# Row blocks 2 and 3, right half, by Strassen instead of plainly, in a fused matmul and RMSNorm kernel

## Chip, cores, metric

The kernel runs on one core of a Trainium2 chip (trn2). The metric is the device time in microseconds (us) of one execution. Every time quoted for a kernel is a median of runs.

In this kernel TensorE (PE in the traces) does the matmuls, ScalarE (ACT) and VectorE (DVE) the copies, sums, squares and scalings, GpSimd (POOL) issues nearly all loads, and SyncE (SP) the DMA transposes and nearly all stores. "Granted clock" is the share of its full clock that the trace records for TensorE. A bank is a piece of the memory into which matmuls accumulate.

## The reference

```python
def setup_inputs():
    m, k, n = 2048, 2048, 2048
    return {"a": randn(m, k), "b": randn(k, n), "gamma": randn(n), "eps": 1e-5}   # float32

def reference(a, b, gamma, eps):
    x = np.matmul(a, b)
    rms = np.sqrt(np.mean(x ** 2, axis=-1, keepdims=True) + eps)
    return (gamma * x / rms).astype(np.float32)
```

## The kernel before

The 2048 rows of the output are 16 row blocks of 128 rows. Its 2048 columns are four chunks of 512; chunks 0, 1 are the left half, 2, 3 the right half.

- **Head.** Row blocks 0 to 3 are multiplied plainly in bf16 while B streams in: the left halves in a first pass, the right halves in a second one.
- **Groups.** Row blocks 4 to 15 are six groups `g = 2..7` of two blocks. A group is done in two half-groups (`j = 0`, `j = 1`), left and right. Each is a one-level Strassen: 7 products of 8 matmuls instead of 8 products.
- **Preparation.** While a group is multiplied, the two blocks of the next one are loaded, their row norms taken, scaled to fp16 by ScalarE, and transposed by DMA.

The half-group: `hooks` are pieces of other work put between its steps.

```python
def group_half(g, j, hooks):
    ...                                        # x11, x12, x21, x22: chunks of the x tiles of this half
    t = x22
    at_hook(0)
    p2, p5 = new_bank(), new_bank()
    product(g, j, 2, p2)
    c = spare if (g, j) == (G0, 0) else t      # G0 = 2
    nc.scalar.copy(out=c, in_=p2)              # must be done before product 4 adds into p2
    last_squares()
    at_hook(1)
    product(g, j, 5, p5)
    nc.vector.tensor_tensor(out=t, in0=p5, in1=c, op=ALU.add)   # before product 3 adds into p5
    at_hook(2)
    ...                                        # product 1; t = p1 - t
    at_hook(3)
    product(g, j, 4, p2, start=False)
    nc.scalar.copy(out=x21, in_=p2)
    square(rb, x21)
    ...                                        # x11 = t + x21
    at_hook(4)
    product(g, j, 3, p5, start=False)
    nc.scalar.copy(out=x12, in_=p5)
    ...                                        # squares, sums, then products 7 and 6
```

The eight x tiles of the head are used again for the groups: a tile must first be scaled (`finish`) and stored. The loads of the blocks after next are paced:

```python
def x_tile(mb, h):
    ...
        if n < 8:
            slot = n
        else:
            g = n // 4
            slot = ((0, 4, 1, 5), (0, 1, 4, 5))[g // 2 % 2 == 0][n % 4] + 2 * (g % 2)
    ...

def load_after(g, mb):
    wait_for(x_chunk(2 * g + 1, 1)[:, 0:1])    # GpSimd reads one column: waits for x22 of j = 0
    load_block(mb)

def hooks_of(g, j):
    ...
    def apply(mb):
        row_apply(mb)                          # scale to fp16
        transpose_dma(mb)                      # issued by SyncE
    if j == 0:
        if g == G0:
            ...                                # row_factor of blocks 6 and 7, row_norm of 7, apply of 6
            hook(2, finish, 1)
            ...
            hook(4, apply, nxt + 1)
            hook(4, finish, 2)
        else:
            hook(0, row_factor, nxt)
            hook(1, apply, nxt)
            ...
            hook(1, row_norm, nxt + 1)
            hook(4, apply, nxt + 1)
    else:
        ...
        if g + 2 < NG:
            hook(0, load_after, g, nxt + 2)
            hook(0, load_block, nxt + 3)
            hook(5, row_norm, nxt + 2)
```

Of the kernel before, what the change touches and what calls it, by code (L numbers as in the profile page):

```python
# [17 lines left out]
def kernel(  # L18
# [32 lines left out]
    stat_pool = ctx.enter_context(tc.tile_pool(name="stat_pool", bufs=8))  # L51
# [25 lines left out]
    spare = head_at.rearrange("p t r m -> p (t r m)")[:, K:2 * K].bitcast(FP32)[:, 0:CH]  # L77

    def a16_slot(mb):

        if mb < HB + 2:
            return x_slot[HB + 1 + 2 * (mb % 2)].bitcast(FP16)
        flat = head_at.rearrange("p t r m -> p (t r m)").bitcast(FP16)
        return flat[:, (2 + mb % 2) * K:(3 + mb % 2) * K]
# [27 lines left out]

    def load_block(mb):
        a32[mb] = a_pool.tile([P, K], FP32, name="a32")
        nc.gpsimd.dma_start(out=a32[mb], in_=a[mb * P:(mb + 1) * P, :])
# [8 lines left out]
    identity_f = consts.tile([P, P], FP32, name="identity_f")  # L124
# [4 lines left out]
    nc.vector.memset(warm, 0.0)  # L129
    identity = consts.tile([P, P], BF16, name="identity")  # L130
# [43 lines left out]
    def transpose_half(mb, g):  # L174
        bank = ps_t.tile([P, CH], FP32, name="tbank")
# [7 lines left out]
        nc.vector.tensor_copy(out=at(mb)[:, g * 8:(g + 1) * 8, :], in_=view)  # L183
# [8 lines left out]
    def new_msq(mb):  # L192
        msq[mb] = stat_pool.tile([P, NCH + 1], FP32, name="msq")
        n_sq[mb] = 0

    for mb in range(HB):
        new_msq(mb)
        nc.gpsimd.memset(msq[mb][:, NCH:], float(eps))
# [27 lines left out]
    def row_apply(mb):  # L226
        a16[mb] = a16_slot(mb)
        if mb < HB + 2:
            nc.vector.tensor_scalar_mul(out=a16[mb], in0=a32.pop(mb), scalar1=factor.pop(mb))
# [5 lines left out]
    def quarter(g, r, c):  # L235
        return at(2 * g + r)[:, c::2, :]

    def a_sums(g, which):
# [3 lines left out]
        for s in which:  # L242
            x, y, op = terms[s]
            nc.vector.tensor_tensor(out=s_sum[s], in0=x, in1=y, op=op)  # L244
# [11 lines left out]
    def b_sum_7(j, kp):  # L256

        b21, b22 = (b_quarter(j, kp, 1, c) for c in range(2))
        nc.vector.tensor_tensor(out=b21, in0=b21, in1=b22, op=ALU.add)

    def b_sum_6(j, kp):

        b11, b12 = (b_quarter(j, kp, 0, c) for c in range(2))
        nc.vector.tensor_tensor(out=b12, in0=b12, in1=b11, op=ALU.add)

# [6 lines left out]
    def product(g, j, m, bank, start=True):  # L272
        for kp in range(KP):
            lhsT = {3: quarter(g, 0, 0), 4: quarter(g, 1, 1)}[m] if m in (3, 4) else s_sum[m]
            rhs = {1: lambda: sums[j][:, 0, kp, :], 2: lambda: b_quarter(j, kp, 0, 0),
                   3: lambda: sums[j][:, 1, kp, :], 4: lambda: sums[j][:, 2, kp, :],
                   5: lambda: b_quarter(j, kp, 1, 1), 6: lambda: b_quarter(j, kp, 0, 1),
                   7: lambda: b_quarter(j, kp, 1, 0)}[m]()
            nc.tensor.matmul(bank, lhsT[:, kp, :], rhs,  # L279
                             start=(start and kp == 0), stop=(kp == KP - 1),  # L280
                             skip_group_check=not start)
# [5 lines left out]
    def square(mb, src):  # L287
# [3 lines left out]
        nc.scalar.activation(out=sq[:, 0:CH], in_=src, func=ACTF.Square,  # L291
                             scale=inv_sqrt_n, accum_out=msq[mb][:, c:c + 1])
# [40 lines left out]

    def finish(mb, order=(0, 1)):
        if mb not in rms_of:
            take_rms(mb)
        r = inverse(rms_of.pop(mb))
# [15 lines left out]
    def new_bank():  # L353
        return ps_a.tile([P, CH], FP32, name="acc")

    later = ([("b", kp) for kp in range(5)]
             + [("a", HB), ("b", 5), ("b", 6), ("a", HB + 1), ("b", 7)])

    def load_later(n):
        for _ in range(min(n, len(later))):  # L360
            kind, which = later.pop(0)
            load_b(1, which) if kind == "b" else load_block(which)
# [31 lines left out]

    groups1 = [(r, c) for r in range(HB) for c in range(2)][:-1]
    last1 = (HB - 1, 1)
    banks = {}
    for r in range(HB):
        x_tile(r, 0)
    transpose_first()  # L400
    for kp in range(KP):
# [4 lines left out]
        before = [lambda: transpose_head(kp + 1)] if kp + 1 < KP else []  # L406
        stream(groups1, kp, before, len(groups1) + 5 if kp == 0 else None)
# [3 lines left out]
        if kp > 0:  # L411
            b_sums(0, kp - 1)
    load_later(2)
    b_sums(0, KP - 1)


    def prepare(mb):
        row_norm(mb)
        row_factor(mb)
        row_apply(mb)  # L420

    def b_sums_2(kp):
        b_sums_in_place(0, kp)
        b_sums(1, kp)
        if kp + 1 < KP:
            b_sum_7(1, kp)

    r3 = HB - 1
    squares = groups1 + [last1]
    groups2 = [(r, c) for r in range(HB) for c in (2, 3)][:-1]  # L430
    for kp in range(KP):
        load_later(1)
        before = [lambda: transpose_half(HB, 0)] if kp == 6 else []
        if kp == 7:
            before = [lambda: transpose_half(HB, 1)]
        stream(groups2, kp, before)
        square(squares[kp][0], x_chunk(*squares[kp]))
        if kp == 4:
            prepare(HB)
        if kp == 6:  # L440

            prepare(HB + 1)
        elif kp == KP - 1:
            b_sums_in_place(0, kp - 1)
        else:
            b_sums_2(kp)
# [3 lines left out]


    def squares2(r):
        for c in (2, 3):
            square(r, x_chunk(r, c))

    evict(groups2[0:2], ())
    squares2(0)
# [279 lines left out]
```

## Time and profile before

| | before |
|---|---|
| time | 224.42 us (224.33 to 224.44, 3 runs) |
| span of the profiled run | 222.6 us |
| TensorE (PE) busy | 211.1 us |
| last matmul starts | 214.41 us |

From the page of the kernel before, the share of each engine, and two rows of the 40 equal slices (busy tenths of PE, granted clock in tenths):

```profile
PE 211.1 (95%) x1043; PEld 98.6 (44%) x1043; DVE 161.8 (73%) x324; ACT 129.1 (58%) x272; POOL 24.5 (11%) x49
...
PE   7899999999999999999999999999999999999950
...
PEclk9999999999999999999999999999999999999997
```

PE is full from the third slice to the thirty-eighth. The chain that ended last, in order of time (start, length, what), says the same: from 69.41 us on it is one piece of PE.

```profile
67.26 2.16 PE acc L350 x10
69.41 140.08 PE acc L279 x648
209.50 0.02 issue
```

648 matmuls in 140.08 us are 216 ns each. The waits of PE over the whole run (us in total, times, longest) all lie before 25 us:

```profile
PE acc L138 <- DVE sq L129: 1.5, 1, 1.5
PE tbank L148 <- POOL msq L198: 1.2, 1, 1.2
PE acc L350 <- DMA b<-in_b_dram: 0.4, 1, 0.4
PE tbank L382 <- DVE head_at L170: 0.4, 1, 0.4
```

By stretches of time (length, then busy us and instructions of PE, weight loads, VectorE, ScalarE, GpSimd, then clock, DMA share, GB/s), PE is full while VectorE is almost full as well:

```profile
80.00:90.00 10.00, 10.00 (x48) 4.44 (x46) 9.42 (x18) 7.46 (x17) 1.24 (x3) 1.00 0.97 293
90.00:100.00 10.00, 10.00 (x48) 4.57 (x47) 8.68 (x22) 8.50 (x19) 0.00 (x0) 1.00 0.52 206
100.00:110.00 10.00, 10.00 (x48) 4.49 (x46) 9.22 (x16) 8.69 (x19) 0.11 (x1) 1.00 0.79 248
```

The last lines shown are GpSimd's in group 3: the pacing copy is released by VectorE's write of x22 (L525), and the two loads for group 5 follow.

```profile
109.89 0.18 POOL L121 COPY pace<-x 128x1 f32<-128x1 f32 x1 [20.46 <-DVE x L525]
110.44 1.05 POOL L115 DMA_DIRECT2D a<-in_a_dram  x2 [0.37 <-issue]
```

They do not wait for the second transpose of the group, which lands at 116.38 us, 5.9 us after the loads are issued.

### The profile page before, as it was taken

To read this page: it belongs to the slowest core of one execution; us is meant where nothing else is said; L and a number is where in the kernel's file an instruction comes from. 1 tells how busy PE (TensorE), PEld (TensorE's weight loads), DVE (VectorE), ACT (ScalarE), POOL (GpSimd) and SP (SyncE) were. 2 spreads that over 40 slices of the span, in tenths; PEclk is the share of its full clock that TensorE was granted. 3 is DMA by queue.
4 is the path that set the end of the run, shared out by engine and by line. 5 is a ranking of instruction groups with operands and counts; after the bars stand their busy time and mean duration, and the time that the engine had idled before them with its cause. 6 is when DMAs were issued, how large, how long until landed. Compare 5 with 4: busy or idle time off the path is not lost.

```text
span 222.6 us, 3026 instructions
## 1 busy us (share of the span) xinstructions
PE 211.1 (95%) x1043; PEld 98.6 (44%) x1043; DVE 161.8 (73%) x324; ACT 129.1 (58%) x272; POOL 24.5 (11%) x49
## 2 busy tenths in 40 slices
PE   7899999999999999999999999999999999999950
PEld 2445444444454444444444444444444444444430
DVE  2427557983999989978949298837994589587692
ACT  3110002807698895799646985699478954334570
POOL 7534232300000001000100002000200000000000
PEclk9999999999999999999999999999999999999997
DMA  6999999999973499818889259945994794044045
GB/s 184 223 202 209 203 208 211 212 303 259 327 280 159 188 272 292 310 72 226 276 228 400 58 174 222 366 151 143 246 368 168 97 282 189 0 188 193 0 190 188
DMA packets 36176, 47.13 MB, mean 212 GB/s; under 512 B 21952, under 2 KB 26048, under 8 KB 34496
## 3 DMA queue, kind: packets, MB, share of 16 engines
q0 software_dynamic: 9648, 23.33, 41.6%
q1 hardware_dynamic: 26080, 22.29, 33.0%
q10 hardware_dynamic: 432, 1.31, 2.0%
q8 instruction: 8, 0.13, 0.2%
q14 instruction: 8, 0.07, 0.1%
HBM read 34.60 MB, written 16.78 MB: 231 GB/s over the span
## 4 chain that ended last, share of the span: by engine, by line
PE 83%; DMA 8%; DVE 2%; POOL 2%; issue 1%; ACT 1%; DVEq 0%; ACTq 0%; POOLq 0%
PE acc L279 63%; PE acc L350 18%; DMA b<-in_b_dram 8%; POOL early L106 1%; DVE x L617 1%; POOL b L100 1%; DVE x L620 1%; PE tbank L179 1%; PE tbank L382 1%; PE tbank L165 1%; ACT sq L291 0%; DVEq L732 0%; ACT sq L682 0%; DVE x L690 0%; DVE r L322 0%
## 5 line engine op out<-in xcount | busy, mean ns | idle before, releaser
L279 PE MATMUL acc<-b,s 128*128 128x512 bf16 x376 | 83.3, 379 | 0.0
L279 PEld LDWEIGHTS <-s 128*128 128x128 f16 x472 | 46.2, 98 | 55.7 <-DVE s L244 0.2
L350 PE MATMUL acc<-b,head_at 128*128 128x512 bf16 x240 | 55.1, 379 | 0.6 <-DMA b<-in_b_dram 0.4
L291 ACT ACTIVATE sq<-x 128x512 bf16<-128x512 f32 x62 | 39.1, 631 | 10.9 <-DVE x L520 5.1
L340 DVE SCALAR_TENSOR_TENSOR x<-x,r,gamma_sb 128x1024 f32<-128x1024 f32 x28 | 34.7, 1282 | 0.8
L209 ACT ACTIVATE sq<-a 128x1024 bf16<-128x1024 f32 x24 | 25.4, 1057 | 16.8 <-DMA a<-in_a_dram 16.4
L350 PEld LDWEIGHTS <-head_at 128*128 128x128 bf16 x240 | 22.9, 98 | 26.7 <-issue 1.1
L393 ACT COPY x<-acc 128x512 f32<-128x512 f32 x11 | 5.9, 591 | 25.1 <-PE acc L350 25.1
L231 ACT ACTIVATE head_at<-a,s 128x2048 f16<-128x2048 f32 x10 | 19.9, 1990 | 0.0
L279 PEld LDWEIGHTS <-at_even 128*128 128x128 f16 x96 | 9.4, 98 | 11.5 <-issue 0.4
L279 PEld LDWEIGHTS <-head_at 128*128 128x128 f16 x96 | 9.4, 98 | 11.3
L100 POOL DMA_DIRECT2D b<-in_b_dram x15 | 10.6, 708 | 16.0 <-DMA b<-in_b_dram 13.2
L217 DVE TENSOR_SCALAR s<-norm 128x1 f32<-128x1 f32 x12 | 1.8, 150 | 14.3 <-ACT norm L212 14.2
L244 DVE TENSOR_TENSOR s<-at_even 128x1024 f16<-128x1024 f16 x15 | 9.7, 684 | 2.8 <-DMA at_even<-head_at 2.8
L291 ACT ACTIVATION_READ_ACCUMULATOR sq<-x 128x1 f32 x62 | 11.7, 188 | 0.0
L279 PE MATMUL acc<-t_left,s 128*128 128x512 bf16 x48 | 11.3, 379 | 0.0
L279 PE MATMUL acc<-early,s 128*128 128x512 bf16 x48 | 11.3, 379 | 0.0
L279 PE MATMUL acc<-early,at_even 128*128 128x512 bf16 x48 | 11.0, 379 | 0.0
L279 PE MATMUL acc<-t_left,at_even 128*128 128x512 bf16 x48 | 10.9, 379 | 0.0
L509 ACT COPY x<-acc 128x512 f32<-128x512 f32 x10 | 5.7, 575 | 8.9 <-PE acc L279 8.9
L279 PE MATMUL acc<-t_left,head_at 128*128 128x512 bf16 x48 | 10.8, 379 | 0.0
L279 PE MATMUL acc<-early,head_at 128*128 128x512 bf16 x48 | 10.8, 379 | 0.0
(86 smaller groups left out, 205.8 us busy)
## 6 DMA issues: line engine op xcount, KB each, us to landing
out_dram<-x SPq DMA_DIRECT2D x30, 512.0 KB, 3.1
a<-in_a_dram POOLq DMA_DIRECT2D x12, 1024.0 KB, 8.5
b<-in_b_dram POOLq DMA_DIRECT2D x15, 512.0 KB, 17.1
early<-in_a_dram POOLq DMA_DIRECT2D x7, 256.0 KB, 14.8
early<-in_b_dram ACTq DMA_DIRECT2D x2, 512.0 KB, 5.9
gamma_sb<-in_gamma_dram POOLq DMA_DIRECT2D x1, 1024.0 KB, 19.9
out_dram<-x SPq DMA_DIRECT2D x3, 256.0 KB, 3.5
early<-in_a_dram SPq DMA_DIRECT2D x1, 512.0 KB, 5.7
```

What stands on the lines that cost most here:

```text
L100: nc.gpsimd.dma_start(out=raw[j][kp], in_=b[kp * W2:(kp + 1) * W2, j * HALF:(j + 1) * HALF].rearrange("(t p) n -> p t n", p=P))
L106: nc.gpsimd.dma_start(out=ah(kp), in_=a[0:HB * P, kp * W2:(kp + 1) * W2].rearrange("(r p) k -> p r k", p=P))
L165: nc.tensor.matmul(view[:, t, r, :], ah(kp)[:, r, t * P:(t + 1) * P], identity, is_transpose=True, start=(t == 0 and r == 0), stop=(t == 1 ...
L209: nc.scalar.activation(out=junk, in_=a32[mb][:, h * HALF:(h + 1) * HALF], func=ACTF.Square, scale=2.0 ** -8, accum_out=n2[:, h:h + 1])
L231: nc.scalar.activation(out=a16[mb], in_=a32.pop(mb), func=ACTF.Copy, scale=factor.pop(mb))
L244: nc.vector.tensor_tensor(out=s_sum[s], in0=x, in1=y, op=op)
L279: nc.tensor.matmul(bank, lhsT[:, kp, :], rhs, start=(start and kp == 0), stop=(kp == KP - 1), skip_group_check=not start)
L291: nc.scalar.activation(out=sq[:, 0:CH], in_=src, func=ACTF.Square, scale=inv_sqrt_n, accum_out=msq[mb][:, c:c + 1])
L340: nc.vector.scalar_tensor_tensor(out=x, in0=x, scalar=r, in1=gamma_sb[:, h * HALF:(h + 1) * HALF], op0=ALU.mult, op1=ALU.mult)
L350: nc.tensor.matmul(bank, head_at[:, kt, r, :], head_rhs(c, kt), start=(kt == 0), stop=(kt == KT - 1))
L393: copy(out=x_chunk(*g), in_=banks[g])
L509: nc.scalar.copy(out=x21, in_=p2)
```

## The change

The intent is to save 8 of 928 matmuls of 512 columns (the last eight are run as sixteen of 256): the right half of row blocks 2 and 3, 64 plain matmuls, becomes one more Strassen half of 56. Its products 2, 5 and 1 are streamed with B in the second pass, 4, 3, 7 and 6 follow. To make room in time and memory, more is moved. The core of the diff:

```diff
+def pair_matmul(m, kp): ...            # one matmul of product m of the pair (blocks 2, 3)
 for kp in range(KP):                    # second pass
     load_later(1)
-    stream(groups2, kp, before)         # 7 plain groups a step; the 8th afterwards
+    b_sums(1, kp)
+    stream_right(kp)                    # 4 plain groups, and products 2, 5, 1 of the pair
...                                      # then pair products 4, 3, 7, 6 with the transposes of blocks 4, 5
 def group_half(g, j, hooks):
-    t = x22
+    first = (g, j) == (G0, 0)
+    c, t = (spare if first else (spare[1], spare[1])) if g == G0 else (x22, x22)
     ...                                 # (G0, 0) does product 5 before product 2
 def load_after(g, mb):
-    wait_for(x_chunk(2 * g + 1, 1)[:, 0:1])
+    wait_for(at(2 * g + 3)[:, KT - 1, 0:1])       # the transposed block itself
     load_block(mb)
 ...                                     # g == G0, j == 0 (other hooks left out):
-                hook(2, finish, 1)
-                hook(4, apply, nxt + 1)
-                hook(4, finish, 2)
+                hook(0, finish, 0, (1,))
+                hook(2, apply, nxt)
+                hook(2, finish, 0, (0,))
+                hook(2, apply, nxt + 1)
+                hook(2, pair_sums)
+                hook(2, pair_ends)
+                hook(5, square_half, r2, 1)
+                hook(5, take_rms, r2)
+                hook(5, square_half, r3, 1)
+                hook(7, finish, 1, (1, 0))
```

Cut: five sums of A for the pair, in-place sums of B, the other moved hooks, the square-root table loaded early, A blocks 4 and 5 loaded in halves after all of B, smaller pools. Before, row block 0 was finished ahead of group 2, and blocks 1 and 2 inside its first half-group. After, the finishing of blocks 0 and 1 stands inside that half-group, that of block 2 in the second.

More of the change, by code (lines that the diff above doesn't have):

```diff
@@ L50 @@
     sq_pool = ctx.enter_context(tc.tile_pool(name="sq_pool", bufs=1))
-    stat_pool = ctx.enter_context(tc.tile_pool(name="stat_pool", bufs=8))
+    stat_pool = ctx.enter_context(tc.tile_pool(name="stat_pool", bufs=4))
+    msq_pool = ctx.enter_context(tc.tile_pool(name="msq_pool", bufs=8))
     ps_t = ctx.enter_context(tc.tile_pool(name="ps_t", bufs=1, space=bass.MemoryType.PSUM))
@@ L75 @@
     x_slot = [consts.tile([P, HALF], FP32, name=f"x_{n}") for n in range(8)]
-    spare = head_at.rearrange("p t r m -> p (t r m)")[:, K:2 * K].bitcast(FP32)[:, 0:CH]
+    spare = head_at.rearrange("p t r m -> p (t r m)")[:, K:2 * K].bitcast(FP32)
+    spare = [spare[:, 0:CH], consts.tile([P, CH], FP32, name="t_first")]
     def a16_slot(mb):
-        if mb < HB + 2:
-            return x_slot[HB + 1 + 2 * (mb % 2)].bitcast(FP16)
         flat = head_at.rearrange("p t r m -> p (t r m)").bitcast(FP16)
@@ L111, with load_half @@
     a32 = {}
+    def load_half(mb, h):
+        if h == 0:
+            a32[mb] = a_pool.tile([P, K], FP32, name="a32")
+        nc.gpsimd.dma_start(out=a32[mb][:, h * HALF:(h + 1) * HALF],
+                            in_=a[mb * P:(mb + 1) * P, h * HALF:(h + 1) * HALF])
     def load_block(mb):
@@ L123 @@
     load_head(1)
-    identity_f = consts.tile([P, P], FP32, name="identity_f")
+    identity_f = t_left[:, 2, KP - 1, 0:2 * P].bitcast(FP32)
     make_identity(nc, identity_f)
@@ L129 @@
     nc.vector.memset(warm, 0.0)
+    nc.vector.memset(pace, 1.0)
+    nc.scalar.activation(out=pace, in_=pace, func=ACTF.Sqrt)
     identity = consts.tile([P, P], BF16, name="identity")
@@ L172, with transpose_half @@
     a16 = {}
-    def transpose_half(mb, g):
-        bank = ps_t.tile([P, CH], FP32, name="tbank")
+    def transpose_half(mb, g, own_bank):
+        if own_bank:
+            bank = ps_t.tile([P, CH], FP32, name="tbank")
+        else:
+            bank = ps_a.tile([P, CH], FP32, name="acc")
         view = bank.bitcast(FP16).rearrange("p (g m) -> p g m", m=P)
@@ L182, in transpose_half, with take_transposed @@
             )
-        nc.vector.tensor_copy(out=at(mb)[:, g * 8:(g + 1) * 8, :], in_=view)
+        return view
+    def take_transposed(mb, g, view, copy):
+        copy(out=at(mb)[:, g * 8:(g + 1) * 8, :], in_=view)
     def transpose_dma(mb):
@@ L192, in new_msq @@
     def new_msq(mb):
-        msq[mb] = stat_pool.tile([P, NCH + 1], FP32, name="msq")
+        msq[mb] = msq_pool.tile([P, NCH + 1], FP32, name="msq")
         n_sq[mb] = 0
@@ L197 @@
         new_msq(mb)
+        nc.gpsimd.memset(msq[mb][:, NCH - 1:NCH], 0.0)
         nc.gpsimd.memset(msq[mb][:, NCH:], float(eps))
@@ L235, in quarter, with sum_of, a_sums @@
     def quarter(g, r, c):
+        if g < G0:
+            return head_at[:, c::2, 2 * g + r, :]
         return at(2 * g + r)[:, c::2, :]
-    def a_sums(g, which):
+    def sum_of(g, s):
+        return s_sum[s].bitcast(BF16) if g < G0 else s_sum[s]
+    def a_sums(g, which, lo=0, hi=KP):
         a11, a12, a21, a22 = (quarter(g, r, c) for r in range(2) for c in range(2))
@@ L243, in a_sums @@
             x, y, op = terms[s]
-            nc.vector.tensor_tensor(out=s_sum[s], in0=x, in1=y, op=op)
+            nc.vector.tensor_tensor(out=sum_of(g, s)[:, lo:hi, :], in0=x[:, lo:hi, :],
+                                    in1=y[:, lo:hi, :], op=op)
     def b_quarter(j, kp, r, c):
@@ L254, in b_sums @@
             nc.vector.tensor_tensor(out=sums[j][:, n, kp, :], in0=x, in1=y, op=op)
-    def b_sum_7(j, kp):
-        b21, b22 = (b_quarter(j, kp, 1, c) for c in range(2))
-        nc.vector.tensor_tensor(out=b21, in0=b21, in1=b22, op=ALU.add)
-    def b_sum_6(j, kp):
-        b11, b12 = (b_quarter(j, kp, 0, c) for c in range(2))
-        nc.vector.tensor_tensor(out=b12, in0=b12, in1=b11, op=ALU.add)
     def b_sums_in_place(j, kp):
@@ L270, in b_sums_in_place, with product_matmul, product @@
                                 op=ALU.add)
-    def product(g, j, m, bank, start=True):
-        for kp in range(KP):
-            lhsT = {3: quarter(g, 0, 0), 4: quarter(g, 1, 1)}[m] if m in (3, 4) else s_sum[m]
-            rhs = {1: lambda: sums[j][:, 0, kp, :], 2: lambda: b_quarter(j, kp, 0, 0),
-                   3: lambda: sums[j][:, 1, kp, :], 4: lambda: sums[j][:, 2, kp, :],
-                   5: lambda: b_quarter(j, kp, 1, 1), 6: lambda: b_quarter(j, kp, 0, 1),
-                   7: lambda: b_quarter(j, kp, 1, 0)}[m]()
-            nc.tensor.matmul(bank, lhsT[:, kp, :], rhs,
-                             start=(start and kp == 0), stop=(kp == KP - 1),
-                             skip_group_check=not start)
+    def product_matmul(g, j, m, bank, kp, start=True):
+        lhsT = {3: quarter(g, 0, 0), 4: quarter(g, 1, 1)}[m] if m in (3, 4) else sum_of(g, m)
+        rhs = {1: lambda: sums[j][:, 0, kp, :], 2: lambda: b_quarter(j, kp, 0, 0),
+               3: lambda: sums[j][:, 1, kp, :], 4: lambda: sums[j][:, 2, kp, :],
+               5: lambda: b_quarter(j, kp, 1, 1), 6: lambda: b_quarter(j, kp, 0, 1),
+               7: lambda: b_quarter(j, kp, 1, 0)}[m]()
+        nc.tensor.matmul(bank, lhsT[:, kp, :], rhs,
+                         start=(start and kp == 0), stop=(kp == KP - 1),
+                         skip_group_check=not start)
+    def product(g, j, m, bank, start=True, within={}):
+        for kp in range(KP):
+            for work in within.get(kp, ()):
+                work()
+            product_matmul(g, j, m, bank, kp, start)
     x_half = {}
@@ L291, in square, with square_half @@
         nc.scalar.activation(out=sq[:, 0:CH], in_=src, func=ACTF.Square,
+                             scale=inv_sqrt_n, accum_out=msq[mb][:, c:c + 1])
+    def square_half(mb, h):
+        c = n_sq[mb]
+        n_sq[mb] += 1
+        sq = sq_pool.tile([P, 2 * CH], BF16, name="sq")
+        nc.scalar.activation(out=sq, in_=x_tile(mb, h), func=ACTF.Square,
                              scale=inv_sqrt_n, accum_out=msq[mb][:, c:c + 1])
@@ L332, in rows @@
         return out[mb * P:(mb + 1) * P, lo:hi]
+    inverse_of = {}
     def finish(mb, order=(0, 1)):
-        if mb not in rms_of:
-            take_rms(mb)
-        r = inverse(rms_of.pop(mb))
+        if mb not in inverse_of:
+            if mb not in rms_of:
+                take_rms(mb)
+            inverse_of[mb] = inverse(rms_of.pop(mb))
+        r = inverse_of[mb]
         for h in order:
@@ L354, in new_bank @@
         return ps_a.tile([P, CH], FP32, name="acc")
-    later = ([("b", kp) for kp in range(5)]
-             + [("a", HB), ("b", 5), ("b", 6), ("a", HB + 1), ("b", 7)])
+    later = [("b", kp) for kp in range(KP)] + [("a", n) for n in range(4)]
     def load_later(n):
@@ L361, in load_later @@
             kind, which = later.pop(0)
-            load_b(1, which) if kind == "b" else load_block(which)
+            load_b(1, which) if kind == "b" else load_half(HB + which // 2, which % 2)
     def stream(groups, kp, before=(), when=None):
@@ L393, in evict @@
             copy(out=x_chunk(*g), in_=banks[g])
+    PAIR = G0 - 1
     groups1 = [(r, c) for r in range(HB) for c in range(2)][:-1]
@@ L399 @@
         x_tile(r, 0)
+    early_sums = {4: ((2,), 0, 6), 5: ((5,), 0, 7), 6: ((1,), 0, KP)}
     transpose_first()
@@ L406 @@
         before = [lambda: transpose_head(kp + 1)] if kp + 1 < KP else []
+        if kp in early_sums:
+            before.append(lambda: a_sums(PAIR, *early_sums[kp]))
         stream(groups1, kp, before, len(groups1) + 5 if kp == 0 else None)
@@ L412 @@
             b_sums(0, kp - 1)
+        if 0 < kp < KP - 2:
+            b_sums_in_place(0, kp - 1)
     load_later(2)
-    b_sums(0, KP - 1)
-    def prepare(mb):
-        row_norm(mb)
-        row_factor(mb)
-        row_apply(mb)
-    def b_sums_2(kp):
-        b_sums_in_place(0, kp)
-        b_sums(1, kp)
-        if kp + 1 < KP:
-            b_sum_7(1, kp)
-    r3 = HB - 1
-    squares = groups1 + [last1]
-    groups2 = [(r, c) for r in range(HB) for c in (2, 3)][:-1]
+    squares = groups1 + [last1]
@@ new lines, with pair_matmul, stream_right @@
+    plain = [(r, c) for r in range(2) for c in (2, 3)]
+    pair = {}
+    def pair_matmul(m, kp):
+        if kp == 0:
+            pair[m] = new_bank()
+        product_matmul(PAIR, 1, m, pair[m], kp)
+    def stream_right(kp):
+        order = [(g, kt) for kt in (2 * kp, 2 * kp + 1) for g in plain]
+        if kp in (0, KP - 1):
+            order.sort(key=lambda x: plain.index(x[0]))
+        if kp == KP - 1:
+            for m in (2, 5):
+                pair_matmul(m, kp)
+            pair_matmul(1, kp - 1)
+        for g, kt in order:
+            if kt == 0:
+                banks[g] = new_bank()
+            head_matmul(banks[g], *g, kt)
+        if kp < KP - 1:
+            for m in (2, 5):
+                pair_matmul(m, kp)
+            if kp > 0:
+                pair_matmul(1, kp - 1)
+        else:
+            pair_matmul(1, kp)
@@ L431 @@
     for kp in range(KP):
         load_later(1)
-        before = [lambda: transpose_half(HB, 0)] if kp == 6 else []
-        if kp == 7:
-            before = [lambda: transpose_half(HB, 1)]
-        stream(groups2, kp, before)
+        b_sums(1, kp)
+        stream_right(kp)
         square(squares[kp][0], x_chunk(*squares[kp]))
-        if kp == 4:
-            prepare(HB)
-        if kp == 6:
-            prepare(HB + 1)
-        elif kp == KP - 1:
-            b_sums_in_place(0, kp - 1)
-        else:
-            b_sums_2(kp)
+        if kp > 0:
+            b_sums_in_place(1, kp - 1)
@@ L447 @@
+        if kp == 0:
+            b_sums(0, KP - 1)
+            b_sums_in_place(0, KP - 3)
+        if kp == 1:
+            b_sums_in_place(0, KP - 2)
+            b_sums_in_place(0, KP - 1)
+        if kp == 2:
+            a_sums(PAIR, (2,), 6, KP)
+            a_sums(PAIR, (5,), 7, KP)
+        if kp in (3, 4):
+            a_sums(PAIR, ((7, 6)[kp - 3],))
     nc.gpsimd.dma_start(out=gamma_sb, in_=gamma.partition_broadcast(P))
@@ L449, with turn, pair_sums, pair_ends @@
     load_block(HB + 3)
-    def squares2(r):
-        for c in (2, 3):
-            square(r, x_chunk(r, c))
-    evict(groups2[0:2], ())
-    squares2(0)
-    evict(groups2[2:-1], ())
-    bank = new_bank()
-    for kt in range(KT):
-        if kt in (0, 6):
-            transpose_half(HB + 1, kt // 6)
-            if kt == 0:
-                b_sums(1, KP - 2)
-                b_sum_7(1, KP - 2)
-        head_matmul(bank, r3, 3, kt)
-    evict(groups2[-1:], ())
-    row_norm(HB + 2)
-    a_sums(G0, (2, 5, 1))
-    finish(0, (1, 0))
-    b_sums_2(KP - 1)
-    nc.scalar.copy(out=x_chunk(r3, 3), in_=bank)
-    squares2(1)
+    r2, r3 = HB - 2, HB - 1
+    for r in range(HB):
+        x_tile(r, 1)
+    x11, x12, x21, x22 = (x_chunk(r, c) for r in (r2, r3) for c in (2, 3))
+    nc.scalar.copy(out=x22, in_=pair[2])
+    nc.vector.tensor_tensor(out=x22, in0=pair[5], in1=x22, op=ALU.add)
+    evict(plain, (2, 3))
+    b_sums_in_place(1, KP - 1)
+    product(PAIR, 1, 4, pair[2], start=False)
+    row_norm(HB)
+    row_norm(HB + 1)
+    nc.vector.tensor_tensor(out=x22, in0=pair[1], in1=x22, op=ALU.subtract)
+    row_factor(HB)
+    product(PAIR, 1, 3, pair[5], start=False)
+    row_apply(HB)
+    nc.scalar.copy(out=x21, in_=pair[2])
+    row_factor(HB + 1)
+    row_apply(HB + 1)
+    p7 = new_bank()
+    turned = {}
+    def turn(mb, g):
+        turned[mb, g] = transpose_half(mb, g, g == 0)
+    product(PAIR, 1, 7, p7, within={5: [lambda: turn(HB, 0)]})
+    turn(HB, 1)
+    for g in range(2):
+        take_transposed(HB, g, turned[HB, g], nc.scalar.copy)
+    nc.scalar.copy(out=x12, in_=pair[5])
+    p6 = new_bank()
+    product(PAIR, 1, 6, p6)
+    a_sums(G0, (5,))
+    for g in range(2):
+        turn(HB + 1, g)
+        take_transposed(HB + 1, g, turned[HB + 1, g], nc.vector.tensor_copy)
+    square_half(0, 1)
+    square_half(1, 1)
+    take_rms(0)
+    a_sums(G0, (2, 1))
+    def pair_sums():
+        nc.vector.tensor_tensor(out=x11, in0=x22, in1=x21, op=ALU.add)
+        nc.vector.tensor_tensor(out=x22, in0=x22, in1=x12, op=ALU.add)
+    def pair_ends():
+        nc.vector.tensor_tensor(out=x11, in0=p7, in1=x11, op=ALU.add)
+        nc.vector.tensor_tensor(out=x22, in0=p6, in1=x22, op=ALU.add)
     late = []
@@ L491, in group_half @@
         x11, x12, x21, x22 = (x_chunk(ra, c1), x_chunk(ra, c2), x_chunk(rb, c1), x_chunk(rb, c2))
-        t = x22
+        first = (g, j) == (G0, 0)
+        c, t = (spare if first else (spare[1], spare[1])) if g == G0 else (x22, x22)
         at_hook(0)
         p2, p5 = new_bank(), new_bank()
-        product(g, j, 2, p2)
-        c = spare if (g, j) == (G0, 0) else t
-        nc.scalar.copy(out=c, in_=p2)
+        one, two = ((5, p5), (2, p2)) if first else ((2, p2), (5, p5))
+        product(g, j, *one)
+        nc.scalar.copy(out=c, in_=one[1])
         last_squares()
         at_hook(1)
-        product(g, j, 5, p5)
-        nc.vector.tensor_tensor(out=t, in0=p5, in1=c, op=ALU.add)
+        product(g, j, *two)
+        nc.vector.tensor_tensor(out=t, in0=two[1], in1=c, op=ALU.add)
         at_hook(2)
@@ L550, in hooks_of @@
             if g == G0:
-                hook(0, row_factor, nxt)
+                hook(0, finish, 0, (1,))
+                hook(1, row_norm, nxt)
                 hook(1, row_norm, nxt + 1)
-                hook(1, apply, nxt)
+                hook(1, take_rms, 1)
+                hook(2, row_factor, nxt)
+                hook(2, apply, nxt)
                 hook(2, a_sums, g, (7, 6))
                 hook(2, row_factor, nxt + 1)
-                hook(2, finish, 1)
-                hook(3, squares2, 2)
-                hook(4, apply, nxt + 1)
-                hook(4, finish, 2)
-                hook(6, b_sum_7, 1, KP - 1)
+                hook(2, finish, 0, (0,))
[6 more added lines that the diff above has]
+                hook(7, finish, 1, (1, 0))
             else:
@@ L575, in hooks_of @@
             if g == G0:
-                hook(1, squares2, r3)
-                for kp in range(KP):
-                    hook(2, b_sum_6, 1, kp)
+                hook(2, finish, r2)
             else:
```

## The prediction

> **What bounds it now.** TensorE. The page shows PE busy 211.1 of 222.6 us; the table by stretch has PE busy 10.00 of 10 us everywhere from 30 to 200 us, at granted clock 1.00. The chain of waits is one PE piece from 69.41 us to 209.5 us, 648 matmuls in 140.08 us: 216 ns each. (The Trainium skill, "TensorE: Matmul & The Clock Gate", Back-to-back issue gap, gives N/2.4 + 2.5 ns, 216 ns at N = 512; the trace agrees.) PE's waits are only 3.5 us, all before 25 us. So time falls only by matmuls removed or by waits before 25 us; anything else is free or new stall.
>
> **Removed from PE.** Right half of blocks 2, 3: 64 plain matmuls become 7 products x 8 = 56. Eight matmuls fewer x 216 ns = 1.73 us (0.77%). The 32 identity transposes (0.45 us per 8) stay. The second pass shrinks to 88 matmuls (39.84 to about 58.8 us), then products 4, 3, 7, 6 and transposes; group one should start at about 67.5 us instead of 69.25.
>
> **Added, moved.** VectorE gets 5 A-sums (0.68 us), 6 fp32 128x512 combinations (0.69) and 2 evictions (0.68): about 9 us, less about 1 us from merging 16 B-sums of 0.42 into 8 of 0.68. VectorE is the second limit: busy 9.3, 9.2, 9.4 of 10 us in 60-70, 70-80, 80-90. Part moves into the first pass, where it was 6 to 7 of 10 busy. ScalarE sheds copies and squares, takes two transposes' copies, and loads the square-root table (1.28 us, at 53.55 us) at the start.
>
> **Second pass against DMA.** Transfers to landing, from the trace: right-half B blocks land every 2.5 us at 38.6, 41.1, 43.7, 46.1, 48.6, then (A block 4 no longer between) 51.1, 53.5, 56.0. PE now takes only 2.37 us a step, needing them at 39.8, 42.0, 44.4, 46.8, 49.1, 51.5, 53.9, 56.2: in time, but with 0.2 to 0.4 us to spare at the end. VectorE's sums follow about 1 us ahead of the lagging third product. I expect 0 to 0.4 us lost. A blocks 4, 5 land about 58.5 and 61.1 as before; norms (2.58 us each on ScalarE) and scaling (1.28) reach the transposes just in time.
>
> **First group.** Both norms of blocks 6, 7 stand on ScalarE from about 70 to 75 us, and VectorE waits for the second factor; then come finish, pair combinations and sums. My hand queue puts the second half-group's p5 combination at about 87.4 us, where product 3, which accumulates in that bank, wants it at about 86.6. I expect 0 to 1.2 us of PE stall there or nearby, 0.5 likely. Later groups and the tail are unchanged; the moved row loads do not bound them.
>
> **Sum.** 224.42 - 1.73 + 0.1 (DMA) + 0.5 (VectorE backlog) = **223.3 us**, range 222.4 to 224.7. Faster by over 2%: 1%; within 2%: 98%; slower by over 2%: 1%.
>
> **What would show it.** Right: 8 fewer 512-column matmuls in the groups; the long PE chain starts at about 67.5 us; any new PE waits name VectorE or DMA b between 40 and 95 us, under 1 us in all; PE's last main matmul earlier by the gain; VectorE busier in 20-40 and 50-60 us. One table load instead of two, worth nothing by itself.
>
> **What would make it wrong.** PE waiting for B (landing interval above 2.5 us: each 0.05 us costs up to 0.3); the scaled block 4 or 5 late for its transposes (loss 1 us); the banks of pair products 7 and 6, freed late by VectorE at about 79 us, being those that the next products take (up to 2.7 us, result slower than before); or the backlog being smaller than I count, giving 222.6.

## The result and the profile after

| | before | after |
|---|---|---|
| time, median | 224.38 us (4 runs) | 234.42 us (234.04 to 234.68, 4 runs) |
| span of the profiled run | 222.6 us | 232.9 us |
| last matmul starts | 214.41 us | 224.63 us |

The ratio is 1.0449 (95% interval 1.0434 to 1.0463), slower. A ratio is the mean time of one kernel's fast runs over that of the other's fast runs in the same rounds, so it is not quite the ratio of the medians quoted.

The kernel lost 10 us, and from the page of the kernel after one sees where to look: slices that are not full, the fifteenth and several after it, and one slice of lower clock, the sixteenth.

```profile
PE 213.5 (92%) x1035; PEld 98.1 (42%) x1035; DVE 168.3 (72%) x330; ACT 127.2 (55%) x263; POOL 26.5 (11%) x55
...
PE   7999999999999968989998899979999899999960
...
PEclk9999999999999997999999999999999999999996
```

The waits of PE after:

```profile
PE acc L289 <- ACT x L571: 4.5, 4, 1.6
PE acc L289 <- ACT t_first L571: 3.2, 1, 3.2
PE acc L145 <- DVE pace L135: 1.5, 1, 1.5
PE acc L289 <- DVE x L575: 1.2, 4, 0.3
PE acc L377 <- DMA b<-in_b_dram: 0.5, 1, 0.5
PE tbank L408 <- DVE head_at L177: 0.4, 1, 0.4
```

L571 is ScalarE's copy of p2 into c, L575 VectorE's sum of p5 and c. So PE waits before product 4 once for 3.2 us, in group 2, and before product 4 and again before product 3 four more times, in groups 3 to 6. The stretches:

```profile
80.00:90.00 10.00, 6.84 (x29) 2.80 (x27) 5.91 (x10) 6.40 (x16) 1.23 (x3) 0.92 0.79 199
90.00:100.00 10.00, 10.00 (x44) 4.39 (x43) 7.49 (x12) 3.00 (x7) 0.00 (x0) 0.91 0.97 355
100.00:110.00 10.00, 9.26 (x43) 4.04 (x42) 7.50 (x20) 9.81 (x23) 0.00 (x0) 1.00 0.34 75
```

From 80 to 90 us no engine is full; from 90 to 100 us PE is, but in part at a lower clock, and ScalarE has 3.0 us of work. This is not overload but waiting. The clock falls to 0.92 and 0.91 around the long wait; in the stretch from 88.4 to 91.7 us it is 0.50.

**The wait at 88 us.** PE's timeline (start, length, idle before in brackets):

```profile
83.31 1.89 PE L289 MATMUL acc<-early,s 128*128 128x512 bf16 x8
88.35 5.28 PE L289 MATMUL acc<-early,at_even 128*128 128x512 bf16 x16 [3.16 <-ACT t_first L571]
93.46 7.07 PE L289 MATMUL acc<-b,s 128*128 128x512 bf16 x32
```

After the idle 3.16 us, 16 matmuls take 5.1 us from their first start to the next group's, where 3.45 us are usual: the starts of the first nine are 0.38 to 0.43 us apart, not 0.216. ScalarE, which PE waited for:

```profile
75.69 3.88 ACT L246 ACTIVATE head_at<-a,s 128x2048 f16<-128x2048 f32 x2
79.48 0.56 ACT L582 COPY x<-acc 128x512 f32<-128x512 f32 x1
...
83.65 0.59 ACT L587 COPY x<-acc 128x512 f32<-128x512 f32 x1 [2.85 <-DMA out_dram<-x]
...
86.47 0.20 ACT L341 ACTIVATE rms<-tot 128x1 f32<-128x1 f32 x1 [0.29 <-DVE tot L339]
86.58 1.04 ACT L314 ACTIVATE sq<-x 128x1024 bf16<-128x1024 f32 x1
...
87.72 0.59 ACT L571 COPY t_first<-acc 128x512 f32<-128x512 f32 x1
```

ScalarE stands idle for 2.85 us before the copy of x12 (L587), until an output DMA has landed: the copy's destination still holds the left half of row block 0. VectorE stands for the same store, 2.84 us before its write of x11 (L584). The Trainium skill, "TensorE: Matmul & The Clock Gate", Architectural detail, calls ScalarE's and VectorE's queues strict FIFO; the trace agrees, for the squares that need nothing from that tile come after it. In the kernel before, the copies of x12 (L514) and of the next p2 (L498) ran without any such wait, for row block 0 had landed at 76.13 us:

```profile
82.86 0.56 ACT L514 COPY x<-acc 128x512 f32<-128x512 f32 x1
...
84.26 0.59 ACT L498 COPY x<-acc 128x512 f32<-128x512 f32 x1
```

SyncE's queue shows why the store was late:

```profile
77.70 2.05 SPq L199 DMA_TRANSPOSE head_at<-head_at  x1
79.82 0.97 SPq L370 DMA_DIRECT2D out_dram<-x  x1
```

VectorE had finished the half at 77.70 us, but the transpose of block 6 went first and held the queue until 79.8 us. The store then landed at 83.55 us.

**The waits of groups 3 to 6.** GpSimd in group 3 (the lines that answer to those of before):

```profile
119.21 0.61 POOL L126 CAST pace<-at_even 128x1 f32<-128x1 f16 x1 [31.52 <-DVE x L579]
119.76 1.05 POOL L120 DMA_DIRECT2D a<-in_a_dram  x2
```

The transposed block landed at 119.06 us, and the loads follow it. The view names VectorE as releaser, whose write ended at 119.14 us; but the code waits for the transposed block alone, and in the next group the copy follows the landing by 0.12 us too (145.09 and 145.21 us). The chain of waits from there (a selection) shows a closed loop, from one group's loads to the next group's, without a piece of PE in it:

```profile
119.76 5.93 DMA a<-in_a_dram
...
125.77 1.16 ACT sq L223 x2
126.95 1.16 ACT sq L223 x2
...
132.35 1.05 ACT sq L223 x2
133.43 1.16 ACT sq L223 x2
...
136.19 1.89 ACT head_at L246
...
139.37 5.72 DMA head_at<-head_at
...
146.10 5.97 DMA a<-in_a_dram
```

Load, norms of both blocks, scaling, transpose, next load: 146.10 - 119.76 = 26.3 us. The next turn takes 171.47 - 146.10 = 25.4 us. PE needs 112 x 0.216 = 24.2 us for a group. The late norms hold ScalarE, whose next item is the copy that PE waits for. This holds for groups 4, 5 and 6. The wait of 1.07 us in group 3 is another: there ScalarE had stood 7.23 us, until 96.91 us, for a store of row block 1 whose tile it was to write.

**The account.** From gaps between starts of matmuls in the two traces:

| | us |
|---|---|
| 8 matmuls fewer | -1.73 |
| wait at 88 us | +3.32 |
| the 16 matmuls after it, 5.11 us in place of 3.45, eight of them at half clock | +1.66 |
| waits before products 4 and 3 of groups 3, 4, 5, 6 (1.07, 2.08, 2.22, 1.60) | +6.96 |
| sum | +10.21 |
| start of the last matmul, 224.63 - 214.41 | +10.22 |

(The list of waits has less for groups 3 to 6, 4.5 + 1.2 us, because it counts from the modelled ends of matmuls and not between starts.) An account says where the time is, not why. The experiments are for that.

### The profile page after: what moved, and what is told of

Read it like the earlier page. It is cut to its first block, busy times and chain, and to the rows that moved or that the text cites. A ratio compares the mean times of both kernels' runs of the same rounds, so it can differ in the third digit from the quotient of the medians.

```text
span 232.9 us, 3012 instructions
## 1 busy us (share of the span) xinstructions
PE 213.5 (92%) x1035; PEld 98.1 (42%) x1035; DVE 168.3 (72%) x330; ACT 127.2 (55%) x263; POOL 26.5 (11%) x55
## 4 chain that ended last, share of the span: by engine, by line
PE 16%; DMA 12%; ACT 11%; DVE 6%; issue 5%; DVEq 0%; POOL 0%; ACTq 0%; POOLq 0%; SPq 0%
PE acc L289 16%; DMA a<-in_a_dram 8%; ACT sq L223 5%; DMA head_at<-head_at 2%; DMA at_even<-head_at 2%; DVE x L367 2%; ACT sq L307 2%; ACT head_at L246 2%; DVE x L694 1%; DVE x L697 1%; ACT x L571 1%; DVE x L575 1%; ACT x L582 0%; ACT x L587 0%; DVE x L584 0%
## 5 line engine op out<-in xcount | busy, mean ns | idle before, releaser
L289 PE MATMUL acc<-b,s 128*128 128x512 bf16 x408 | 92.1, 379 | 0.0
L289 PEld LDWEIGHTS <-s 128*128 128x128 f16 (+1 forms) x512 | 49.9, 98 | 59.9 <-DVE s L264 0.4
L377 PE MATMUL acc<-b,head_at 128*128 128x512 bf16 x176 | 41.9, 379 | 0.6 <-DMA b<-in_b_dram 0.5
L307 ACT ACTIVATE sq<-x 128x512 bf16<-128x512 f32 x54 | 34.0, 630 | 10.5 <-DVE x L593 5.0
L377 PEld LDWEIGHTS <-head_at 128*128 128x128 bf16 x176 | 16.8, 98 | 20.2 <-issue 1.4
L289 PEld LDWEIGHTS <-head_at 128*128 128x128 f16 (+1 forms) x112 | 10.9, 98 | 16.5 <-issue 3.8
L289 PE MATMUL acc<-early,head_at 128*128 128x512 bf16 x64 | 14.5, 379 | 0.0
L289 PE MATMUL acc<-early,s 128*128 128x512 bf16 x56 | 14.4, 379 | 0.0
L289 PE MATMUL acc<-t_left,at_even 128*128 128x512 bf16 x48 | 11.2, 378 | 3.0 <-ACT x L571 2.4
L289 PE MATMUL acc<-t_left,head_at 128*128 128x512 bf16 x48 | 11.2, 378 | 2.6 <-ACT x L571 2.0
L264 DVE TENSOR_TENSOR s<-head_at 128x1024 f16<-128x1024 f16 (+5 forms) x22 | 13.5, 640 | 0.1
L582 ACT COPY x<-acc 128x512 f32<-128x512 f32 x10 | 5.8, 576 | 10.9 <-DMA out_dram<-x 7.2
L280 DVE TENSOR_TENSOR b<-b 128x1024 bf16<-128x1024 bf16 x16 | 11.0, 697 | 0.2
```

The source lines that it names most:

```text
L264: nc.vector.tensor_tensor(out=sum_of(g, s)[:, lo:hi, :], in0=x[:, lo:hi, :], in1=y[:, lo:hi, :], op=op)
L280: nc.vector.tensor_tensor(out=flat[:, 1:3, :], in0=flat[:, 1:3, :], in1=flat[:, 0::3, :], op=ALU.add)
L289: nc.tensor.matmul(bank, lhsT[:, kp, :], rhs, start=(start and kp == 0), stop=(kp == KP - 1), skip_group_check=not start)
L307: nc.scalar.activation(out=sq[:, 0:CH], in_=src, func=ACTF.Square, scale=inv_sqrt_n, accum_out=msq[mb][:, c:c + 1])
L377: nc.tensor.matmul(bank, head_at[:, kt, r, :], head_rhs(c, kt), start=(kt == 0), stop=(kt == KT - 1))
```

## The experiments

All kernels gave correct results. "Before" is the kernel before on the same chip in the same rounds: 224.32 us for the first four, 224.28 us for the next four, 224.48 us for the last two.

| run | edit | us | against before |
|---|---|---|---|
| (after) | the change | 234.42 | 1.0449 |
| e1_old_pacing | after, old pacing | 233.06 | 1.0376 |
| e2_before_new_pacing | before, new pacing | 230.31 | 1.0267 |
| e3_early_store | after, row block 0 stored earlier | 234.30 | 1.0441 |
| e4_both | e1 and e3 | 229.81 | 1.0237 |
| e5_own_t | after, another tile for t in (2, 1) | 234.50 | 1.0464 |
| e6_stores_first | e4, row block 1 stored ahead of the loads | 226.09 | 1.0079 |
| e7_stores_first_new_pacing | e6, new pacing | 231.00 | 1.0289 |
| e8_loads_after_stores | e4, loads held until the stores landed | 230.44 | 1.0285 |
| e9_t_group3 | e6, spare tile for t in (3, 0) | 222.98 | 0.9933 |
| e10_square_later | e9, one square later | 222.53 | 0.9913 |

### Old pacing in the changed kernel

```diff
-        wait_for(at(2 * g + 3)[:, KT - 1, 0:1])
+        wait_for(x_chunk(2 * g + 1, 1)[:, 0:1])
```

> The changed kernel, with only the pacing of the row loads put back (loads of the next two blocks wait for the last column of the first half-group's x22 and not for the landed transposes). Theory P (pacing): the new wait closes a loop (load, norm, scale, transpose, load) that takes 25.4 to 26.3 us a group where TensorE needs 24.2, and its PE waits in the third to fifth groups (2.1 + 2.2 + 1.6 us by the trace) go: about 228.5 us, range 227.5 to 229.5. Rival K (knock-on): those waits are only lateness inherited from the 3.2 us stall at 88 us: pacing changes little, 233 us or more. The 3.2 us stall at 88 us stays under both.

Measured: 233.06 us (232.31 to 233.75), a miss for P's number and close to K's. Yet the trace shows that P's waits are gone: PE has none after 110 us. In their place group 3 has one wait of 3.4 us at 106 us, after ScalarE had stood 8.73 us for a store, and eight or nine matmuls at about half the clock behind it. So pacing was a cause, but not the only one, and taking it away laid bare another.

### New pacing in the kernel before

```diff
-        wait_for(x_chunk(2 * g + 1, 1)[:, 0:1])
+        wait_for(at(2 * g + 3)[:, KT - 1, 0:1])
```

> The kernel before, with only the new pacing. Theory P: PE waits of 1 to 2 us appear before the fourth product of the groups from the third on, and the time rises by 2 to 5 us, to 226.5 to 229.5 us. Rival K: nothing to inherit here, so 224.4 us within 0.5.

Measured: 230.31 us (229.54 to 231.29), 6.0 us more than before; a little over P's range, and far from K's 224.4. PE's waits in groups 4, 5 and 6, which the kernel before did not have (L498 is the copy of p2, L502 the sum of p5):

```profile
PE acc L279 <- ACT x L498: 3.9, 3, 2.6
...
PE acc L279 <- DVE x L502: 0.6, 2, 0.3
```

The loop is there again: loads at 114.10, 139.48 and 165.71 us, 25.4 and 26.2 us apart. The three waits before product 4 grow, 0.2, 1.1 and 2.6 us, which fits a loop of 25 to 26 us that first eats its slack and then falls behind 24.2 us a group. The last wait is followed by eight matmuls at 0.43 us, which I had not counted. The pacing alone costs 6 us: shown.

### Row block 0's left half stored earlier

```diff
+                hook(2, finish, 0, (0,))
                 hook(2, row_factor, nxt)
                 hook(2, apply, nxt)
                 hook(2, a_sums, g, (7, 6))
                 hook(2, row_factor, nxt + 1)
-                hook(2, finish, 0, (0,))
```

> The changed kernel, with only the scaling of the left half of row block 0 moved ahead of the scaling of block 6, so that its store is issued before the transposes of block 6 and not behind them. Theory S: the stall at 88 us comes from ScalarE waiting 2.9 us to write x12 over that half until its store has landed (83.55 us); the store lands near 76.5 us instead, the 5.0 us lost there (3.3 wait, 1.7 at half clock) shrink to about 1.1, and with the new pacing kept the later groups still lose: 230 us, range 229 to 231.5. Rival K: the later waits go as well, 225 us or less. If S is wrong: 234 us.

Measured: 234.30 us (233.04 to 235.37): no gain, by the number the case "S is wrong". The trace says otherwise. The store lands at 75.7 us, ScalarE no longer waits for it, and PE's wait before product 4 falls from 3.16 to 0.03 us; before product 3, 0.6 us are left. What was won is lost 14 us later, where ScalarE waits for the next output tile:

```profile
94.94 0.59 ACT L582 COPY x<-acc 128x512 f32<-128x512 f32 x1 [8.71 <-DMA out_dram<-x]
```

PE then waits 4.1 us at 102 us, and half clock follows. Here the total alone would have led to the wrong verdict; the wait had moved.

### Both

> The changed kernel with the old pacing and the early store together. P and S both right: 224.4 - 1.7 for eight matmuls + 1.1 left in the second half-group = 223.8 us, range 222.8 to 225. If the sum falls short of the two single effects, they share a cause.

Measured: 229.81 us (228.69 to 230.39), a miss by 6 us. But 4.6 us below the changed kernel, where the single edits gave 1.4 and 0.1: the two defects covered each other, the opposite of a shared cause. PE's waits left are 0.5 and 0.6 us in group 2 and 4.3 us in group 3. The stores of row block 1 explain the last, from the times of issue and landing in the trace:

```
e4_both: issue, landing, us between
 85.53   91.22   5.69  load of block 8        86.05   95.61   9.55  load of block 9
 86.36   95.77   9.41  store, block 1 right   87.56   98.31  10.76  store, block 1 left
```

### Rival for the wait at 88 us: the temporary

The wait names `t_first`, the spare tile that both half-groups of group 2 use for t in the changed kernel. A write-after-read on it (the copy may not write the tile before the last reader of its old content is done) would look the same.

```diff
+    t_second = ...                       # part of a scaled block that is dead by then
-        c, t = (spare if first else (spare[1], spare[1])) if g == G0 else (x22, x22)
+        c, t = (spare if first else (t_second, t_second)) if g == G0 else (x22, x22)
```

> The changed kernel, with another place for the temporary t of the second half-group alone, so that its first copy need not wait until the first half-group has used its t. Rival W: the stall at 88 us, which the profile puts down to that temporary, is this write-after-read: it goes, and 3 to 5 us with it. Theory S: ScalarE is only free at 87.7 us anyway, the temporary at 87.6: no change, 234.4 within 1.

Measured: 234.50 us (234.37 to 235.29), no change; the wait is 2.9 us in place of 3.2. So the tile that the list of waits names is not the cause by itself. ScalarE's queue, held up by the store, is: run three moved the store and the wait went.

### Row block 1 stored ahead of the loads

```diff
-                hook(7, finish, 1, (1, 0))
+                hook(3, finish, 1, (1, 0))       # on top of e4_both
```

> Old pacing and early store (the fourth run), and the finishing of row block 1 moved from the end of the first half-group to just after its first subtraction, so that its two stores are issued before the loads of blocks 8 and 9. Theory C (collision): the 4.3 us stall at 103 us of the fourth run is ScalarE waiting for those stores to land, which takes 9.4 and 10.8 us beside the loads, against 2.6 to 3.8 us alone; here they land before 88 us, both stalls go, and the kernel comes to 224.4 - 1.7 + 0.3 = 223.0 us (222.5 to 224), below the kernel before. Rival: the stall has another cause, and the time stays near 229 us.

Measured: 226.09 us (225.34 to 226.46). The cause was right and the size was not: 3.7 us of gain instead of 6.8. The two stores now land at 85.3 and 86.7 us, after 3.5 and 3.8 us, and ScalarE's wait for them is gone. A third one shows, for the stores of row block 2, issued at 87 and 88 us behind the loads:

```profile
97.67 0.59 ACT L571 COPY x<-acc 128x512 f32<-128x512 f32 x1 [4.12 <-DMA out_dram<-x]
```

### The same with the new pacing

> The sixth run with the new pacing again: theory P says that the loop alone costs here what it cost the kernel before (6 us): 229 us, range 227.5 to 230.5. If the stores alone were at fault: 223 us.

Measured: 231.00 us (230.01 to 231.49), 4.9 us more than with the old pacing, just above the range. PE's waits before product 4 in groups 4, 5 and 6 are back, 2.0, 1.3 and 1.1 us. With the second run this shows the pacing's cost in two settings, 6.0 and 4.9 us.

### Loads held until the stores have landed

```diff
         wait_for(x_chunk(2 * g + 1, 1)[:, 0:1])        # on top of e4_both
+        if g == G0:
+            for r in (2 * g + 1, 2 * g):
+                nc.gpsimd.memset(x_tile(r, 1)[:, 0:1], 0.0)
```

> The fourth run with the loads of blocks 8 and 9 held back until the two stores of row block 1 have landed, order and arithmetic untouched (one column that is overwritten later is cleared to make the wait). Theory C: stores land in about 3 us, the 4.3 us stall and its slow clock go; the loads land near 96 and 100 us, which costs some 1 us by the norms: 225 us, range 224 to 227. Rival (the stores are late for another reason): later loads can only add, 230 us or more.

Measured: 230.44 us (229.75 to 232.03), a miss. The mechanism is there: the same two stores, issued alone, land in 2.65 and 2.72 us instead of 9.41 and 10.76, and PE's wait in group 3 is 2.1 instead of 4.3 us. But the loads go out at 91.6 us instead of 85.5, and the lateness is paid with interest: PE waits 2.9 us at 124 us for VectorE's sums of the next group's transposed blocks, and the half clock follows. The second of these blocks landed only at 123.20 us, its transpose having taken 10.4 us beside the next two loads. So stores and loads do collide, a transpose beside loads is slow too, but holding the loads is no remedy. The order to seek is stores first and loads not later.

### The third store wait

```diff
-        c, t = (spare if first else (spare[1], spare[1])) if g == G0 else (x22, x22)
+        c, t = (spare if first else (spare[1], spare[1])) \
+            if (g, j) in ((G0, 0), (G0, 1), (G0 + 1, 0)) else (x22, x22)     # on top of e6
```

> The sixth run, and the first half of group three keeps its temporary t in the spare tile and not in x22. Theory C again: the wait left at 98 us (0.9 + 0.3 us) is ScalarE's copy into x22, held until the stores of row block 2, issued at 87 and 88 us behind the loads, have landed (97.6 us); it also makes the scaling of block 8, and so the transposes that the 0.8 us wait at 119 us is for, late. All three go: 226.1 - 2.4 = 223.7 us, and as a distance from the kernel before -0.3 to -1.4 us. Rival: the copy is late because of the norms of block 8 before it on ScalarE: no change.

Measured: 222.98 us (222.66 to 223.31), ratio 0.9933 (0.9921 to 0.9946). All three waits of PE went, though the stores still take 8.8 us beside the loads: nobody needs them that early any more. This is below the kernel before, by 1.5 us, a little more than expected.

### One square later

```diff
-                hook(5, square_half, r3, 1)            # g == G0, j == 0
+                hook(1, square_half, r3, 1)            # g == G0, j == 1; this half-group uses t_second
```

> The ninth run, and the squares of row block 3's right half moved behind the first copy of the second half-group, which gets a temporary of its own. It aims at the 0.2 to 0.5 us wait at 85 us alone: 0.2 to 0.5 us below the ninth run, near 224.4 - 1.7 = 222.7 to 223.2 us. If the ninth run hides a wait that follows, no gain.

Measured: 222.53 us (222.40 to 222.73), ratio 0.9913 (0.9900 to 0.9927), 0.45 us below the ninth run; but the wait that it aimed at cost only 0.24 us in the trace of run nine, and the two intervals overlap, so a gain beyond that is not shown. PE's waits:

```profile
PE acc L146 <- DVE pace L136: 1.5, 1, 1.5
PE tbank L156 <- POOL msq L213: 0.8, 1, 0.8
PE acc L378 <- DMA b<-in_b_dram: 0.5, 1, 0.5
PE tbank L409 <- DVE head_at L178: 0.3, 1, 0.3
```

They are those of the start again, and none comes after 25 us. The last matmul starts at 212.69 us, 1.72 us before that of the kernel before, where 8 x 0.216 is 1.73. In time it is 1.95 us (1.64 to 2.24, from the interval). The Strassen part of the change is worth what the sum gave it, once the rest is put right.

## Why the prediction was wrong

- **Right: what bounds, and what is saved.** PE bound the kernel before, and eight matmuls are worth 1.73 us. The tenth run has 1.72 us of it in the trace. The Trainium skill, "TensorE: Matmul & The Clock Gate", Back-to-back issue gap, gives the prediction's formula for an isolated matmul, and about 131 ns a matmul for a sustained stream at N = 512; the 648 matmuls in a row of the trace of before took 216 ns each, so here the measurement speaks for the formula.
- **Right: the second pass and the DMA of B.** I predicted its end at about 58.8 us and the start of group 2 at about 67.5 us; the trace of after has 58.92 and 67.66. B came in time.
- **Too small, and for another cause: "I expect 0 to 1.2 us of PE stall there or nearby, 0.5 likely."** The place was right, the second half-group of group 2 (the prediction's first group), but partly by luck: forecast was VectorE late with p5 before product 3, and PE waited for ScalarE's copy of p2 before product 4. The size was 3.3 us and 1.7 us more of half clock. The forecast wait does exist: it shows, with 0.6 us, once the store is out of the way (run three). I counted the work on ScalarE and VectorE and took the store of row block 0 for landed when the copy into its tile was due. It was queued 2.1 us behind a transpose on SyncE, took 3.7 us to land, and ScalarE stood 2.85 us before that copy. The third run removed that wait; the fifth ruled out the temporary by itself.
- **The step that failed: "Later groups and the tail are unchanged; the moved row loads do not bound them."** They bound them: the waits of groups 4 to 6 in the trace of after are 5.9 of the 10.2 us. The loads were made to wait for the transposes, which closes load, norm, scaling, transposing into one loop of 25.4 to 26.3 us a group against 24.2 us of PE. Alone it costs 6.0 us in the kernel before and 4.9 us in the sixth run. I had looked at the edit for what it frees and not for the length of the loop that it closes, though every duration in it was in the trace of before: a load 6 us, two norms 5.1 us, a scaling 1.9 us, a transpose some 5 us. These make only 18 us; the other 7 to 8 us are the first block's scaling and the copies and squares that stand between them on ScalarE's queue.
- **Not foreseen: stores beside loads.** Stores of 512 KB that land in 2.6 to 4.5 us away from loads take 7.6 to 11.4 us when two 1 MB loads are issued just before. The kernel before has such stores too (8.3 to 11.2 us from group 3 on), and they cost it nothing: PE never waits after 25 us, since no engine needs those tiles so soon. The change put the finishing of row blocks 1 and 2 next to the loads of blocks 8 and 9, and into tiles that are written again soon. In the changed kernel this was mostly hidden behind the wait at 88 us and the pacing (1.07 us showed, in group 3); each fix uncovered it (runs one, three, four), and moving the stores or the temporary away from it closed it (runs six and nine).
- **Where a late store's time goes.** The Trainium skill, "DMA: Bandwidth & Descriptors", Queues, rings and completion order, says that a DMA engine takes packets of its queues in turn; the packet records in the trace of run four agree for the later part only. From 90.9 to 94 us the load queue has 97 packets of data and the store queue 94. But from the first store's issue at 86.36 us until 90.9 us there are 151 of loads and none of stores, while in run eight, without loads beside it, the same store's first packet comes 0.83 us after its issue. So 3.7 of the 6.8 us by which this store is later lie before its first packet. The loads suffer little: they land in 5.7 and 9.6 us there (the second in 10.2 to 10.9 us in runs six, seven, nine and ten), and in 5.9 and 9.4 us without stores beside them (after, at 119.76 us). Why the stores' packets start so late is not shown.
- **Not foreseen: the price of a long wait.** A wait of 2.6 us or more was followed each time by some eight matmuls at about 0.43 us, some 1.7 us more; the clock record has 0.5 for 3.4 us each time.

What stays open: whether a point between the old pacing and the new one would be better than both was not tried. With the old pacing the second transpose of group 3 takes 7.7 to 8.3 us beside the loads (10.4 us in run eight), with the new one 5.1 us; the change probably aimed at that, which I can't show.

## What to carry to other kernels

When a wait is moved, lay out the loop that it closes, from one turn to the next, and compare its length with the time of the bounding engine for one turn; each step may be hidden and the loop still too long. Before putting a buffer to a second use, follow its last store to its landing, with the queue in front of it and the loads beside it, since an in-order engine that waits for it holds up everything behind. And when a fix gains nothing, read the trace before dropping it: here two right fixes gained 1.4 and 0.1 us alone, and 4.6 us together.

## What the Trainium skill lacked or had wrong

- "TensorE: Matmul & The Clock Gate", Part 1: it gives about 3.4 us of idle time for the fall to half clock (and about 3 us in its advice). Here idle waits, counted from the modelled end of the last matmul, of 2.6 us (run two), 2.9 us (runs five and eight) and 3.2 us (after) already brought a granted clock of 0.5 and matmuls 0.43 us apart, eight or so, about 1.7 us each time; waits of 2.0 and 2.1 us (runs seven and eight) did not.
- "DMA: Bandwidth & Descriptors" tells how long an on-chip transpose keeps its sequencer only for 8,192 tiles, in the comparison with trn3. Here transposes of a 128 x 2048 fp16 block held SyncE's queue for 1.7 to 3.6 us each, and in after a store that was ready waited 2.05 us behind one.
- "DMA: Bandwidth & Descriptors" gives no figure for stores beside loads: 512 KB stores landed in 2.6 to 4.5 us away from loads and in 7.6 to 11.4 us when issued just behind two 1 MB loads; the first packet of such a store in group 2 came 4.2 to 4.5 us after its issue, against 0.83 us in run eight.
